# A shorter GpSimd chain, its powers queued on VectorE, the up projection's operands by halves, and the conditioning's rows written as rows

## The chip, the cores and the metric

One Trainium2 core runs the kernel. The metric is the device time in microseconds (us) of one execution. The engines named below are TensorE (PE in the profile), VectorE (DVE), ScalarE (ACT), GpSimd (POOL) and SyncE (SP), which issues most loads. Each engine runs its own instructions strictly in order; semaphores tie the engines together. ScalarE and GpSimd also issue DMAs (ACTq and POOLq in the profile), in the same order as their other instructions.

## The reference

One layer of a decoder trunk, on 1024 tokens of 1024 channels in float32. The conditioning vector c gives six rows of 1024 (shift, scale and gate, twice).

```python
ada = silu(c) @ w_ada + b_ada
sh1, sc1, g1, sh2, sc2, g2 = split(ada, 6)
h = modulate(x, sh1, sc1)
proj = h @ w_in
(xc, gc, gb, u_ssm, c_q, c_kv, k_r, g_conv, g_ssm, g_attn) = split(proj)
y_conv = (gb * causal_conv3(gc * xc)) @ w_up_conv
y_ssm  = glu(gelu(ssm(u_ssm))) @ w_up_ssm      # complex diagonal recurrence
y_attn = mla(c_q, c_kv, k_r, cos, sin) @ w_up_attn
y = (sigmoid(g_conv)*y_conv + sigmoid(g_ssm)*y_ssm + sigmoid(g_attn)*y_attn) @ w_o
x = layer_norm(a * x + g1 * y)
y = grouped_moe(modulate(x, sh2, sc2))
x = layer_norm(a * x + g2 * y)
```

The state-space branch has 32 groups of 64 complex states. Its step is lambda = exp(a*dt), a magnitude times (cos, sin) of an angle. The rotary tables cos and sin are of positions times inverse frequencies.

## The kernel before

A float32 product is made of three TensorE products of split operands (`mm3`, L137: low weights by high data, L140; high by low, L141; high by high, L142). `split_into` (L121) makes the high part by a cast on ScalarE (L125) and the low part by a subtraction on VectorE (L129). A projection tile of 128 channels by 1024 tokens is two halves of 512, each of 24 such matmuls.

The stages on TensorE follow each other in this order. The **front** (L480) normalises and modulates x and at once projects three of the four tiles of u, the state-space input; its order on VectorE, ScalarE and TensorE is written out by hand. `high(j)` (L570) makes the eight modulated slices on ScalarE, `low(j)` their low parts on VectorE. Behind it the **state-space stage** runs: u's tile 3 and five attention gates are projected (`proj_u`, `gates_att`), and between their matmuls stand the small ones of four quarters q of the state space (`s5_prep`, `s5_run`), of which each needs tables from GpSimd (X, T) and VectorE (G), a scan on VectorE and result rows Y that ScalarE takes from PSUM and SyncE writes to the array ys. Then `proj_qkv` (L876) projects the rotary key kr and the three tiles cq0 to cq2; its evacuation writes the buffers nt1, nt2 and nt3, and a table ctab is loaded from the array csd. Gates 5 to 7, moving sums and the paired projections follow (to about 585 us), then the **branches** (L1083: up projections of the convolution and the state space, with the rest of the conditioning's rows summed as they go by, `ada_rest`), attention, the merge, and the experts.

`s5_params` (L757) is GpSimd's long chain beside the front. It takes the exponentials of the step, one sine and cosine of 144 angles per partition (`sincos`: 16 of the state space and 128 of the rotary tables together), writes the rotary part to csd by four DMAs on ScalarE's queue (L789), makes lambda and the input factors, and squares the step's phase eight times (z8, L808 to L817). `s5_prep` makes a table T of 128 powers by seven doublings, six operations each, on GpSimd.

Outside the front and other stretches written by hand, a scheduler decides the order of each engine's instructions. The source order, the tile pools and `issue_after` (nothing of what follows is queued ahead of a given instruction) bound its choice. So the instruction order is shown below with the change.

## Time and profile before

| | us |
|---|---|
| median of 3 runs | 1539.91 (1537.67 to 1541.26) |
| profiled execution | 1540.56 |
| its span, first to last instruction | 1538.8 |
| TensorE busy | 1399.5 (91%) |
| VectorE busy | 914.3 (59%) |
| ScalarE busy | 483.4 (31%) |
| GpSimd busy | 373.6 (24%) |

TensorE is busy for nine tenths of the span, but its busy time is not the same as full speed: the mean clock granted to it is 0.960, and in single stretches it is 0.50. What other engines cost is therefore read from TensorE's waits and from the stretches behind them in which it runs at half clock.

### The profile page before, as it was taken

What the parts mean: (1) busy time and instruction counts of PE and PEld (TensorE: products, weight loads), DVE (VectorE), ACT (ScalarE), POOL (GpSimd) and SP (SyncE); (2) the same over time, 40 slices, a digit from 0 to 9 for tenths busy, and PEclk for the clock granted to TensorE, in tenths of its full rate; (3) what the DMA queues carried; (4) which work ended last, traced back from release to release, by engine and by line L of the source; (5) the groups of instructions that cost most, each with busy time, mean ns of one, the idle gap of its engine ahead of it and who ended that gap; (6) DMA issues with size and microseconds to landing.
All of it is one profiled execution on the core that took longest, in us unless ns stands there. A gap on an engine that the chain in (4) does not pass through costs nothing. (4 is left out here: it accounts for less than half of the span.)

```text
span 1538.8 us, 19602 instructions
## 1 busy us (share of the span) xinstructions
PE 1399.5 (91%) x6934; PEld 998.5 (65%) x6934; DVE 914.3 (59%) x1608; ACT 483.4 (31%) x869; POOL 373.6 (24%) x571
## 2 busy tenths in 40 slices
PE   4599797999999998999799997899988999999966
PEld 2477676888888886787587885688987333333322
DVE  7464687568765547557477887978886111122128
ACT  5232113522233334121367774333511111111103
POOL 7999930000000000004511143510032111111110
PEclk9899998999999998999899998999999999999988
DMA  9232222312133348869500005644635799778726
GB/s 371 104 117 85 77 56 42 122 64 83 55 109 110 110 151 329 249 203 215 84 1 15 15 22 188 206 172 172 250 139 200 276 340 347 289 264 308 239 104 259
DMA packets 78056, 251.61 MB, mean 164 GB/s; under 512 B 15946, under 2 KB 27266, under 8 KB 68739
## 3 DMA queue, kind: packets, MB, share of 16 engines
q1 hardware_dynamic: 54096, 203.61, 38.3%
q10 hardware_dynamic: 15506, 25.73, 4.8%
q0 software_dynamic: 8352, 20.98, 4.7%
q8 instruction: 56, 0.92, 0.2%
q14 instruction: 46, 0.37, 0.1%
HBM read 302.53 MB, written 50.38 MB: 229 GB/s over the span
## 5 line engine op out<-in xcount | busy, mean ns | idle before, releaser
L1143 POOL TENSOR_TENSOR mg<-mg,sg 128x512 f32<-128x512 f32 x16 | 22.5, 1418 | 491.1 <-DMA raw<-krd 474.6
L140 PE MATMUL ps_mm<-hh,wlo 128*128 128x512 f32 x304 | 123.0, 405 | 9.4 <-DVE nt L895 8.6
L1636 PE MATMUL ps_h<-wo,xt 128*64 128x512 f32 x480 | 130.9, 596 | 0.0
L142 PE MATMUL ps_mm<-hh,whi 128*128 128x512 f32 x304 | 123.3, 405 | 0.0
L141 PE MATMUL ps_mm<-hl,whi 128*128 128x512 f32 x304 | 122.5, 403 | 0.0
L1629 ACT COPY xt<-ps_tr 128x512 f32<-128x512 f32 x48 | 28.1, 585 | 244.8 <-PE ps_tr L1627 244.8
L1636 PE MATMUL ps_y<-wo,ht 128*64 128x512 f32 x288 | 87.6, 598 | 0.0
L1636 PE MATMUL ps_h<-ql,xt 128*64 128x512 f32 x192 | 87.0, 596 | 0.0
L125 ACT CAST whi<-raw 128x1024 fp32r<-128x1024 f32 (+1 forms) x45 | 46.8, 1040 | 126.6 <-PE ps_up L142 82.7
L129 DVE TENSOR_TENSOR wlo<-raw,whi 128x1024 fp32r<-128x1024 f32 x44 | 60.2, 1369 | 43.2 <-ACT whi L125 43.2
L1689 DVE TENSOR_TENSOR hd<-ps_h,hd 128x256 f32<-128x256 f32 x24 | 10.2, 424 | 126.9 <-ACT hd L1688 126.9
L140 PEld LDWEIGHTS ps_mm<-hh,wlo 128*128 128x128 f32 x304 | 58.8, 193 | 23.2 <-DVE nt L895 8.8
L1636 PEld LDWEIGHTS ps_h<-wo,xt 128*64 128x64 f32 x480 | 38.6, 137 | 49.6 <-issue 49.4
L142 PEld LDWEIGHTS ps_mm<-hh,whi 128*128 128x128 f32 x304 | 58.8, 193 | 14.6 <-issue 1.3
L141 PEld LDWEIGHTS ps_mm<-hl,whi 128*128 128x128 f32 x304 | 58.7, 193 | 13.3 <-issue 0.2
L1607 POOL DMA_INDIRECT xg<-h2d,idx x26 | 26.4, 1014 | 166.4 <-PE ps_tr L1627 137.4
L140 PE MATMUL ps_up<-ah,wlo 128*128 128x512 f32 x128 | 52.5, 418 | 10.1 <-ACT ah L125 7.5
L1664 DVE SCALAR_TENSOR_TENSOR y<-ps_y,roww,g 128x512 f32<-128x512 f32 x48 | 36.0, 751 | 38.8 <-PE ps_y L1636 38.8
L1249 DVE TENSOR_REDUCE sm<-ps_S 128x1 f32<-128x256 f32 (+3 forms) x64 | 49.2, 770 | 11.9 <-PE ps_S L1246 11.1
L129 DVE TENSOR_TENSOR pl<-ps_T,ph 128x512 fp32r<-128x512 f32 (+1 forms) x80 | 45.9, 580 | 14.5 <-ACT ph L125 13.2
L140 PE MATMUL ps_mm<-wo,ml 128*128 128x512 f32 x128 | 50.2, 400 | 3.1 <-DVE sg L1359 3.1
L141 PE MATMUL ps_up<-al,whi 128*128 128x512 f32 x128 | 52.0, 406 | 0.0
(676 smaller groups left out, 3878.8 us busy)
## 6 DMA issues: line engine op xcount, KB each, us to landing
wo<-exp SPq DMA_DIRECT2D x110, 1024.0 KB
qh<-exp SPq DMA_DIRECT2D x26, 1024.0 KB
ql<-exp SPq DMA_DIRECT2D x26, 1024.0 KB
raw<-w_in SPq DMA_DIRECT2D x43, 512.0 KB
adr<-w_ada SPq DMA_DIRECT2D x32, 512.0 KB
wada<-w_ada SPq DMA_DIRECT2D x16, 512.0 KB
fy<-yd SPq DMA_DIRECT2D x16, 512.0 KB
sga<-sg ACTq DMA_DIRECT2D x8, 512.0 KB
```

The lines of the kernel that those rows point to most:

```text
L125: nc.scalar.copy(out=hi, in_=src)
L129: e.tensor_tensor(out=lo, in0=src, in1=hi.bitcast(F32), op=ALU.subtract)
L140: mm(ps, wl, xh, start=first, stop=False)
L141: mm(ps, wh, xl, start=False, stop=False)
L142: mm(ps, wh, xh, start=False, stop=last)
L1143: nc.gpsimd.tensor_tensor(out=mg[m][:, sl], in0=mg[m][:, sl], in1=sg[:, sl], op=ALU.add)
L1249: v.tensor_reduce(out=sm[:], in_=x, axis=AX.XY if two else AX.X, op=ALU.max, negate=True)
L1607: self.nc.gpsimd.indirect_dma_start(out=self.xg[b % 2][:], out_offset=None, in_=self.h2d[:], in_offset=bass.IndirectOffsetOnAxis(ap=self.i ...
L1629: self.nc.scalar.copy(out=self.ex[b][:, n * 512:(n + 1) * 512], in_=ps[:])
L1636: self.nc.tensor.matmul(ps[z * 64:(z + 1) * 64, :], x[:, z * 64:(z + 1) * 64], w[z], start=first, stop=last, tile_position=(0, 64 * z))
L1664: nc.vector.scalar_tensor_tensor(out=y[:, sl], in0=ps[:], scalar=self.roww[:, b:b + 1], in1=self.g2[:, sl], op0=ALU.mult, op1=ALU.mult)
L1689: v.tensor_tensor(out=hd[:], in0=ps[:, 256:], in1=hd[:], op=ALU.mult)
```

## The change

It has six parts.

1. The 128 rotary angles leave the chain of `s5_params`: its sine and cosine have 16 columns. A new function `rotary`, called behind `s5_run(1)`, makes the tables on GpSimd in two buffers of u's ring (uq) and writes csd by four DMAs on GpSimd's own queue.
2. The powers z8 move from GpSimd to VectorE, behind the front's last `low`. Two small tables join them there: za (16 powers) and zb (8 powers), by four and three doublings.
3. T is one complex product of za and zb, six operations of 128x512, in place of seven doublings.
4. The evacuation of kr uses a ring of its own instead of nt1 and nt2, whose use stood behind ctab.
5. In the branches the first up weights are loaded and split ahead of the operands; the four operands are cast by halves, the very first half on VectorE; what follows is queued behind these casts until m is 1.
6. Each conditioning column [128, 8] is transposed on TensorE, copied by ScalarE to 8 rows of 128, and written as 8 rows of 512 bytes instead of 1024 single elements.

```diff
--- before
+++ after
                             prep.append(self.s5_prep(q + 2))
+                        if q == 1:
+                            self.rotary()
                     if self.stop == "s5":
...
             self.ada_col(col[:], self.aacc, 2 + c)
-            self.nc.scalar.dma_start(out=self.adad[c].rearrange("(j p) -> p j", p=128), in_=col[:])
+            ps, row = self.ps("mm"), P.tile([8, 128], F32, name="arow", tag="arow", bufs=2)
+            self.nc.tensor.transpose(ps[0:8, 0:128], col[:], self.ident[:])
+            self.nc.scalar.copy(out=row[:], in_=ps[0:8, 0:128])
+            self.nc.scalar.dma_start(out=self.adad[c].rearrange("(j p) -> j p", p=128), in_=row[:])
...
             for sl in (slice(0, 512), slice(512, S)) if j == 0 else (slice(0, S),):
-                v.tensor_tensor(out=self.hl[j][:, sl], in0=hts[j][:, sl], in1=self.hh[j][:, sl].bitcast(F32), op=ALU.subtract)
+                self.front_end = v.tensor_tensor(out=self.hl[j][:, sl], in0=hts[j][:, sl], in1=self.hh[j][:, sl].bitcast(F32),
+                                                 op=ALU.subtract).ins
...
         bb = self.bb
-        pos = P2.tile([128, 128], I32, name="pos")
-        nc.scalar.dma_start(out=pos[:], in_=bass.AP(a["positions"].tensor, 0, [[0, 16], [128, 8], [1, 128]]))
-        invf = t_("invf", 1)
-        nc.scalar.dma_start(out=invf[:], in_=a["inv_freq"])
         ar, ai, ldt = par[:, 0], par[:, 1], par[:, 2]
...
         self.exp_small(mag[:], t16[:], P2, [128, 16], v)
-        ang = t_("ang", 144)
-        v.tensor_tensor(out=ang[:, :16], in0=ai, in1=dt[:], op=ALU.mult)
-        v.tensor_copy(out=ang[:, 16:], in_=pos[:])
-        v.tensor_scalar(out=ang[:, 16:], in0=ang[:, 16:], scalar1=invf[:], scalar2=None, op0=ALU.mult)
-        sn, cs = t_("sn", 144), t_("cs144", 144)
-        self.sincos(sn[:], cs[:], ang[:], P2, [128, 144], v)
-        nsn = t_("nsn", 128)
-        v.tensor_scalar(out=nsn[:], in0=sn[:, 16:], scalar1=-1.0, scalar2=None, op0=ALU.mult)
-        csd = self.csd = self.dram.tile([2, 32, S], F32, name="csd")
-        for dst, src in ((csd[0, 0:16], cs[:, 16:]), (csd[0, 16:32], cs[:, 16:]), (csd[1, 0:16], nsn[:]),
-                         (csd[1, 16:32], sn[:, 16:])):
-            nc.scalar.dma_start(out=dst.rearrange("f (b t) -> (f b) t", b=8), in_=src)
+        ang = t_("ang", 16)
+        v.tensor_tensor(out=ang[:], in0=ai, in1=dt[:], op=ALU.mult)
+        sn, cs = t_("sn", 16), t_("cs16", 16)
+        self.sincos(sn[:], cs[:], ang[:], P2, [128, 16], v)
...
             v.tensor_tensor(out=self.m8[:], in0=self.m8[:], in1=self.m8[:], op=ALU.mult)
+        d = nc.vector
+        behind = ExitStack()
+        behind.enter_context(self.tc.issue_after(self.front_end))
         z = f("z8", 8, 2, 16)
-        v.tensor_copy(out=z[:, 0, 0], in_=cs[:, :16])
-        v.tensor_copy(out=z[:, 0, 1], in_=sn[:, :16])
+        d.tensor_copy(out=z[:, 0, 0], in_=cs[:, :16])
+        d.tensor_copy(out=z[:, 0, 1], in_=sn[:, :16])
+        self.za, self.zb = f("za", 2, 16, 16), f("zb", 2, 16, 8)
+        zt = t_("zt", 16, 8)
+        for x in (self.za, self.zb):
+            d.memset(x[:, 0, :, 0:1], 1.0)
+            d.memset(x[:, 1, :, 0:1], 0.0)
+        def double(x, n, i):
+            self.cmul(x[:, 0, :, n:2 * n], x[:, 1, :, n:2 * n], x[:, 0, :, 0:n], x[:, 1, :, 0:n],
+                      bc(z[:, i, 0], 2, n), bc(z[:, i, 1], 2, n), zt[:, :, :n], d)
         for i in range(9):
             src, dst = max(0, i - 3), max(0, i - 2)
             s0, s1, d0, d1 = z[:, src, 0], z[:, src, 1], z[:, dst, 0], z[:, dst, 1]
-            v.tensor_tensor(out=z[:, 7, 0], in0=s0, in1=s0, op=ALU.mult)
-            v.tensor_tensor(out=z[:, 7, 1], in0=s1, in1=s1, op=ALU.mult)
-            v.tensor_tensor(out=d1, in0=s0, in1=s1, op=ALU.mult)
-            v.tensor_scalar(out=d1, in0=d1, scalar1=2.0, scalar2=None, op0=ALU.mult)
-            v.tensor_tensor(out=d0, in0=z[:, 7, 0], in1=z[:, 7, 1], op=ALU.subtract)
+            d.tensor_tensor(out=z[:, 7, 0], in0=s0, in1=s0, op=ALU.mult)
+            d.tensor_tensor(out=z[:, 7, 1], in0=s1, in1=s1, op=ALU.mult)
+            d.tensor_tensor(out=d1, in0=s0, in1=s1, op=ALU.mult)
+            d.tensor_scalar(out=d1, in0=d1, scalar1=2.0, scalar2=None, op0=ALU.mult)
+            d.tensor_tensor(out=d0, in0=z[:, 7, 0], in1=z[:, 7, 1], op=ALU.subtract)
+        for n, i in ((1, 0), (2, 1), (4, 2), (8, 3)):
+            double(self.za, n, i)
+        for n, i in ((1, 4), (2, 5), (4, 6)):
+            double(self.zb, n, i)
         self.z8 = z
+        behind.close()
...
+    def rotary(self):
+        nc, a, v = self.nc, self.a, self.nc.gpsimd
+        us = [self.uqp.tile([128, 8, 128], F32, name="uq", tag="uq", bufs=2) for _ in range(2)]
+        room = [us[i // 8][:, i % 8] for i in range(16)]
+        names = {}
+        class P:
+            tile = staticmethod(lambda shape, dt, name, tag: names.setdefault(tag, room[len(names)]))
+        pos, ang, sn, cs = (P.tile(None, F32, n, n) for n in ("pos", "ang", "sn", "cs"))
+        pos = pos.bitcast(I32)
+        nc.scalar.dma_start(out=pos[:], in_=bass.AP(a["positions"].tensor, 0, [[0, 16], [128, 8], [1, 128]]))
+        invf = self.cst.tile([128, 1], F32, name="invf")
+        nc.scalar.dma_start(out=invf[:], in_=a["inv_freq"])
+        v.tensor_copy(out=ang[:], in_=pos[:])
+        v.tensor_scalar(out=ang[:], in0=ang[:], scalar1=invf[:], scalar2=None, op0=ALU.mult)
+        self.sincos(sn[:], cs[:], ang[:], P, [128, 128], v)
+        csd = self.csd = self.dram.tile([2, 32, S], F32, name="csd")
+        put = lambda dst, src: nc.gpsimd.dma_start(out=dst.rearrange("f (b t) -> (f b) t", b=8), in_=src)
+        put(csd[0, 0:16], cs[:])
+        put(csd[0, 16:32], cs[:])
+        put(csd[1, 16:32], sn[:])
+        v.tensor_scalar(out=ang[:], in0=sn[:], scalar1=-1.0, scalar2=None, op0=ALU.mult)
+        put(csd[1, 0:16], ang[:])
     def proj_u(self):
...
                                      stop=k == KT - 1 and i == 1)
-            t, k = half("nt1"), half("nt2")
+            x = self.ring("kr")
+            t, k = x[:, 0:512], x[:, 512:1024]
             nc.scalar.copy(out=t[0:64, :], in_=ps[64:128, :])
...
         T = f("T", 2, 4, 128, bufs=3)
-        tt = f("tt", 4, 64)
-        gp.memset(T[:, 0, :, 0:1], 1.0)
-        gp.memset(T[:, 1, :, 0:1], 0.0)
-        n, i = 1, 0
-        while n < 128:
-            self.cmul(T[:, 0, :, n:2 * n], T[:, 1, :, n:2 * n], T[:, 0, :, 0:n], T[:, 1, :, 0:n],
-                      bc(self.z8[:, i, 0, pr], 2, n), bc(self.z8[:, i, 1, pr], 2, n), tt[:, :, :n], gp)
-            n, i = 2 * n, i + 1
+        tb = lambda x: x.rearrange("p g (b a) -> p g b a", b=8)
+        za = lambda z: bc(self.za[:, z, pr], 2, 8)
+        zb = lambda z: bc(self.zb[:, z, pr], 3, 16)
+        self.cmul(tb(T[:, 0]), tb(T[:, 1]), zb(0), zb(1), za(0), za(1), tmp[:], gp)
...
-        if m % 2 == 0:
+        if m % 2 == 0 and self.upw is None:
             raw = self.load(src[m // 2].rearrange("p m k f -> p (m k f)"))
             self.upw = self.split(raw)
-        wh, wl = (w[:, (m % 2) * 512:(m % 2 + 1) * 512] for w in self.upw)
+        upw, self.upw = self.upw, None if m % 2 else self.upw
+        wh, wl = (w[:, (m % 2) * 512:(m % 2 + 1) * 512] for w in upw)
         for n in range(2):
...
         mg = [P.tile([128, S], F32, name=f"mg{m}") for m in range(KT)]
-        for t in range(4):
-            self.split_into(ah[t], al[t], self.load(self.cvd[t])[:])
+        self.upw = self.split(self.load(self.a["w_up_conv"][0].rearrange("p m k f -> p (m k f)")))
+        raws = [self.load(self.cvd[t]) for t in range(4)]
+        for n in range(2):
+            sl = slice(n * 512, (n + 1) * 512)
+            for t in range(4):
+                if n == t == 0:
+                    v.tensor_copy(out=ah[t][:, sl], in_=raws[t][:, sl])
+                else:
+                    hi = nc.scalar.copy(out=ah[t][:, sl], in_=raws[t][:, sl])
+                lo = v.tensor_tensor(out=al[t][:, sl], in0=raws[t][:, sl], in1=ah[t][:, sl].bitcast(F32), op=ALU.subtract)
+        behind = ExitStack()
+        for i in (hi, lo):
+            behind.enter_context(self.tc.issue_after(i.ins))
...
                 gelu(m // 2)
+            if m == 1:
+                behind.close()
         z = self.zp.tile([128, 4, S], F32, name="z")
```

(In the rows that follow, line numbers above the change's first hunk agree in both kernels, later ones are shifted: L577 and L583 are both `high`, L585 and L591 both `low`, L457 and L459 the same sigmoid, L1107 and L1155 the same gelu.)

**ScalarE at the end of the front.** Before, the four writes of csd stand between the sixth slice and the last two (hh_188 is slice 5's high part, hh_497 slice 6's); two of them are queued ahead of slice 6's `high`:

```order
L581 CAST hh_188<-ht 128x1024 [waits Activation_49]
L789 DMA csd<-sn 128x128 [waits DMAHW2_49,Pool_49]
L789 DMA csd<-nsn 128x128 [waits DMAHW3_49,Pool_49]
L577 ACTIVATE ht<-ps_x,col 128x512 [waits DVE_49,PE_49]
L577 ACTIVATE ht<-ps_x,col 128x512 [waits PE_49]
L789 DMA csd<-cs_662 128x128 [waits DMAHW4_49,Pool_49]
L789 DMA csd<-cs_662 128x128 [waits DMAHW5_49]
L581 CAST hh_497<-ht 128x1024 [waits PE_49]
L577 ACTIVATE ht<-ps_x,col 128x512 [waits DVE_49]
```

With the change the same place reads:

```order
L583 ACTIVATE ht<-ps_x,col 128x512 [waits DVE_49,PE_49]
L583 ACTIVATE ht<-ps_x,col 128x512 [waits PE_49]
L587 CAST hh_497<-ht 128x1024 [waits PE_49]
L583 ACTIVATE ht<-ps_x,col 128x512 [waits DVE_49]
L583 ACTIVATE ht<-ps_x,col 128x512 [waits PE_49]
L587 CAST hh_535<-ht 128x1024 [waits Activation_49]
L901 COPY uq<-ps_mm 128x8x64 [waits PE_49] x2
```

Slices 6 and 7 follow slice 5 directly, and no instruction there waits for GpSimd.

**VectorE behind the front.** hl_498 and hl_536 are the low parts of slices 6 and 7, wlo the low weights of u's tile 3, G a table of the state space. Before:

```order
L560 TENSOR_TENSOR col<-col,bias_180 128x2 [waits DVE_49]
L585 TENSOR_TENSOR hl_498<-ht,hh_497 128x1024 [waits PE_49,Activation_49]
L585 TENSOR_TENSOR hl_536<-ht,hh_535 128x1024 [waits PE_49,Activation_49]
L129 TENSOR_TENSOR wlo<-raw,whi 128x1024 [waits DMAHW2_49,PE_49,Activation_49]
L750 TENSOR_TENSOR G<-lam,cc 128x512 [waits DVE_49,Pool_49]
```

With the change, the rows from the last two low parts on:

```order
L591 TENSOR_TENSOR hl_498<-ht,hh_497 128x1024 [waits PE_49,Activation_49]
L591 TENSOR_TENSOR hl_536<-ht,hh_535 128x1024 [waits PE_49,Activation_49]
L805 COPY z_744<-cs_656 128x16 [waits Pool_49]
L806 COPY z_744<-sn 128x16
L811 MEMSET za 128x16
L812 MEMSET za 128x16
L811 MEMSET zb 128x16
L812 MEMSET zb 128x16
L820 TENSOR_TENSOR z_744<-z_744 128x16 [waits DVE_49]
```

and, 43 rows of the same kind further, the last ones ahead of tile 3's weights:

```order
L757 TENSOR_TENSOR za<-za,z_744 128x16x4
L824 TENSOR_TENSOR z_744<-z_744 128x16 [waits DVE_49]
L760 TENSOR_TENSOR za<-za,z_744 128x16x4
L823 TENSOR_SCALAR z_744<-z_744 128x16 [waits DVE_49]
L762 TENSOR_TENSOR za<-za,zt 128x16x2 [waits DVE_49]
L129 TENSOR_TENSOR wlo<-raw,whi 128x1024 [waits DMAHW1_49,PE_49,Activation_49]
```

The weights that TensorE needs for u's tile 3 now stand behind 55 small operations, of which the first waits for GpSimd's cosine.

**ScalarE where the branches begin.** sg is a gate's sigmoid, cv the gelu of a state-space row block, ah the high part of the convolution's operand. Before:

```order
L457 ACTIVATE sg<-sg 128x512 [waits DVE_49]
L1107 ACT_TABLE_LOAD [waits DMAHW3_49]
L1107 ACTIVATE cv<-raw 128x1024 [waits PE_49]
L1107 ACTIVATE cv<-raw 128x1024 [waits DMAHW6_49]
L459 DMA sgs<-sg 128x1024 [waits Activation_49]
L125 CAST ah<-raw 128x1024 x3
L125 CAST ah<-raw 128x1024 [waits DMAHW0_49]
```

With the change:

```order
L459 ACTIVATE sg<-sg 128x512 [waits DVE_49]
L461 DMA sgs<-sg 128x1024 [waits DMAHW6_49,Activation_49]
L1144 CAST ah<-raw 128x512 [waits PE_49]
L1144 CAST ah<-raw 128x512 [waits DMAHW4_49]
L1144 CAST ah<-raw 128x512 [waits DMAHW5_49]
L1144 CAST ah<-raw 128x512 x4
L1155 ACT_TABLE_LOAD
L1155 ACTIVATE cv<-raw 128x1024 [waits PE_49]
L1155 ACTIVATE cv<-raw 128x1024 [waits DMAHW2_49]
```

The seven half casts stand ahead of the activation table's load and the gelus.

## Rows read from the trace of the kernel before

**Rows 1.** Waits of TensorE, whole span: total, times, longest (us).

```profile
PE ps_x L568 <- ACT ht L577: 17.7, 2, 16.5
...
PE ps_mm L140 <- DVE nt L895: 8.6, 1, 8.6
...
PE ps_up L140 <- ACT ah L125: 7.5, 1, 7.5
PE ps_ss L972 <- POOL X L755: 6.1, 1, 6.1
PE ps_S L140 <- DVE qf L1214: 5.9, 1, 5.9
...
PE ps_up L140 <- DVE sg L1142: 2.6, 2, 2.0
```

**Rows 2.** Timeline of ScalarE, 72 to 80 us: start, duration, instruction, idle before.

```profile
74.42 0.78 ACT L577 ACTIVATE ht<-ps_x,col 128x512 f32<-128x512 f32 x1 [22.83 <-DMA csd<-sn]
```

**Rows 3.** Timeline of GpSimd, 38 to 75 us.

```profile
38.32 1.07 POOL L694 CAST ki<-k 128x16 int32<-128x16 f32 x1
...
58.67 0.22 POOL L691 TENSOR_TENSOR p<-p,r 128x16 f32<-128x16 f32 x1
...
74.24 0.49 POOL L746 TENSOR_TENSOR cs<-c,p 128x144 f32<-128x144 f32 x1
```

**Rows 4.** Timeline of TensorE at u tile 3's start, 88 to 91 us.

```profile
90.15 0.50 PE L140 MATMUL ps_mm<-hh,wlo 128*128 128x512 f32 x1 [0.79 <-DVE wlo L129]
```

**Rows 5.** Timeline of VectorE, 88 to 103 us.

```profile
88.42 1.67 DVE L129 TENSOR_TENSOR wlo<-raw,whi 128x1024 fp32r<-128x1024 f32 x1 [7.03 <-ACT whi L125]
90.02 0.70 DVE L750 TENSOR_TENSOR G<-lam,cc 128x512 f32<-128x512 f32 x1
...
100.68 2.19 DVE L755 TENSOR_TENSOR G<-G,xg 128x512 f32<-128x512 f32 x1
```

**Rows 6.** Groups of VectorE by shape, 0 to 60 us: busy us, mean ns, idle before.

```profile
L541 DVE TENSOR_TENSOR lnst<-lnst 128x2 f32<-128x2 f32 x2 | 0.3, 160 | 0.1
```

**Rows 7.** Timeline of VectorE in the state-space stage.

```profile
140.50 0.69 DVE L1025 TENSOR_TENSOR w<-ps_ss,T 128x512 f32<-128x512 f32 x1 [9.19 <-POOL T L752]
...
206.10 0.68 DVE L1025 TENSOR_TENSOR w<-ps_ss,T 128x512 f32<-128x512 f32 x1
...
230.27 0.69 DVE L755 TENSOR_TENSOR s<-s,xw 128x508 f32<-128x508 f32 x1
```

**Rows 8.** Timeline of TensorE in the state-space stage.

```profile
194.66 1.23 PE L1050 MATMUL ps_ss<-s,G 64*128 64x128 f32 x8
...
214.69 0.40 PE L140 MATMUL ps_mm<-hh,wlo 128*128 128x512 f32 x1
214.92 0.39 PE L141 MATMUL ps_mm<-hl,whi 128*128 128x512 f32 x1
...
243.97 0.80 PE L140 MATMUL ps_mm<-hh,wlo 128*128 128x512 f32 x1 [8.61 <-DVE nt L895]
```

**Rows 9.** Timeline of ScalarE where the branches begin.

```profile
588.07 3.79 ACT L1107 ACTIVATE cv<-raw 128x1024 f32<-128x1024 f32 x2
591.77 3.87 ACT L125 CAST ah<-raw 128x1024 fp32r<-128x1024 f32 x4
```

**Rows 10.** One stretch there: us, busy (x instructions) of PE, PEld, DVE, ACT, POOL; PEclk, DMA share, GB/s.

```profile
592.00:597.00 5.00, 4.14 (x9) 2.89 (x10) 5.00 (x5) 3.64 (x4) 0.00 (x0) 0.50 1.03 420
```

**Rows 11.** Two stretches behind the conditioning's writes, columns as above.

```profile
704.00:712.00 8.00, 8.00 (x37) 6.50 (x37) 7.96 (x8) 0.83 (x1) 5.60 (x6) 1.00 1.10 98
739.00:745.00 6.00, 5.44 (x24) 4.08 (x22) 1.21 (x2) 0.48 (x1) 1.98 (x3) 1.00 1.50 41
```

**Rows 12.** Timeline of ScalarE's DMA queue around the last of these writes.

```profile
738.99 0.37 ACTq L478 DMA_DIRECT2D adad<-acol  x1
...
744.57 1.10 ACTq L1176 DMA_DIRECT2D tab<-csd  x2
```

**Rows 13.** Timeline of VectorE at attention's start.

```profile
755.48 0.69 DVE L1214 TENSOR_TENSOR qf<-ps_S,tab 128x512 f32<-128x512 f32 x1 [5.89 <-DMA tab<-csd]
```

More of the change, by code (lines that the diff above doesn't have):

```diff
@@ L171, in build @@
             tc = self.tc
-            self.pst_ = None
+            self.pst_ = self.upw = None
             pool = lambda st, name, **kw: st.enter_context(tc.tile_pool(name=name, bufs=1, reuse_waits="tile", **kw))
```

## The prediction

> **What bounds the kernel now.** TensorE is busy for 1399.5 of 1538.8 us, so I read its waits first, then what the instruction behind each wait was itself waiting for, and last the stretches that follow, because TensorE often comes back from a wait at half clock. Six waits belong to places that the diff touches [rows 1]: 16.5 us in the front for `high`'s ht, 8.6 us for kr's nt, 7.5 us for the up projection's operand ah, 6.1 us for a table X of GpSimd, 5.9 us for a query qf, and 2.6 us for gates sg. The longest is not ScalarE's own work: its `high` started at 74.42 after 22.83 us of idleness that a DMA of csd ended, whose source is the sine [rows 2]. GpSimd's cosine came at 74.24 + 0.49 = 74.73 [rows 3]. So the front is bound by GpSimd's chain, through a queue and not through data.
>
> The wait for nt ends at 243.97 [rows 8], 13.0 us behind the last scan product of the fourth quarter (230.27 + 0.69 = 230.96, [rows 7]). The wait for ah ends behind two gelus of 3.79 us and the first of four casts of about 1 us [rows 9]. The one for qf ends with the table read from csd, issued at 744.57 and landed by 755.48 [rows 12, 13].
>
> **The change part by part: front.** No csd DMA stands ahead of slices 6 and 7 any more. TensorE's front ended 0.79 us before 90.15, at 89.4 [rows 4]; without the 16.5 us it ends at about 73. That gain doesn't pass on whole, for u's tile 3 needs its low weights, and these now stand on VectorE behind 55 small operations, the first of which needs GpSimd's cosine. When does that come? GpSimd's 128x16 operations take 0.22 us alone against 0.49 for 128x144, but 1.07 us beside VectorE's large ones [rows 3]. Some 31 wide operations lay in the uncontended part (about 57 to 74.7 us): 31 x 0.27 = 8.4 us less, 66.3. The two `low`s now fall into it (2 x 1.2 us in which GpSimd may be held up), so between 65 and 69; I take 67. The nearest rows to the 55 operations are VectorE's small ones of 160 ns with 0.05 us between them [rows 6]: 55 x 0.21 = 11.6 us, then the weights at 1.67 us [rows 5]. That gives 80.3. If GpSimd's own small operations were to alternate with them throughout, each would cost 0.21 + 0.22 and the start would be 67 + 23.7 + 1.7 = 92. I take 82, near the uncontended end, because a 16-column operation is short, and keep 79 to 92 for the range. Tile 3 then starts 8 us earlier than at 90.15.
>
> **State-space stage.** Here I count matmuls in the instruction order, from tile 3's first to the first quarters' last result: before, 275 wide ones and 147 others by the end of quarter 1's Y at 195.9 [rows 8]; now 332 and 179, because more of the filler is queued ahead. A wide one takes 0.23 us (214.92 - 214.69, [rows 8]): 0.2335 over longer stretches. Before: 195.9 - 90.15 = 105.7 us, less 64.2 for the wide ones and less the 6.1 us for X, leaves 35.4 us, 0.24 for each other one, small waits included. Now: 82 + 77.5 + 43 = 202.5. To this comes whatever TensorE waits for X. T's seven doublings (42 operations a quarter) become six operations of 128x512 at about 1.2 us, but some 80 rotary operations of 128x128 are queued between them, and VectorE no longer waits 9.19 us for the first T [rows 7]. GpSimd's load in this stage is therefore about the same, and I charge 3 us, with 0 and 10 as bounds: 205.5. Behind it the chain is serial as before: 2 us for the third quarter's state products, then VectorE's two quarters, which ran from 206.10 to 230.96 (24.9 us, [rows 7]), then 13.0 us until nt: 205.5 + 2 + 24.9 + 13.0 = 245.4. This wait stays in the program: with the change it is nt3 of cq2 that stands behind ctab on ScalarE. But kr's and cq1's matmuls are queued ahead of it, since kr no longer uses nt1 and nt2. That is 48 more wide matmuls than before, 11.2 us. The old kernel was at that point of its work at 243.97 + 11.2 = 255.2. **Gain of front and state space: about 10 us**; bounds 0 (tile 3 at 92) and 18 (tile 3 at 79, no X wait, and the chain covered so that only the 8.6 us remain).
>
> **csd and kr.** csd's four writes now wait on GpSimd's queue behind the rotary operations. ctab needs them. Its own wait for ys ended at about 242 before, and GpSimd's last work in this stage came earlier, so I charge nothing; if GpSimd ran late this cover would go, which is the slow rival below.
>
> **Branches.** The half casts move ahead of the table load and the gelus. The first half is on VectorE, free at once after the last gate; so the first up matmul waits about 1 us instead of 7.5. The stretch behind the wait ran at clock 0.50 for some 5 us [rows 10], a loss of about 2.4 us; a shorter pause should spare most of it. Against this, ScalarE's half casts (about 0.6 us by half of the row of rows 9) and the low parts pace the first sixteen products, and the gelus come later, but their results are wanted only behind the convolution's up projection. I take 8 us, with 4 and 10 as bounds.
>
> **Conditioning's rows.** Behind two of the four writes of single elements the DMA engines are full and move little: busy share 1.10 at 98 GB/s, then 1.50 at 41 GB/s [rows 11], against 420 GB/s in a full stretch [rows 10]. The last of them was issued at 738.99 on the same queue as the table, 5.6 us ahead of it [rows 12]; VectorE stood idle for 5.89 us until the table was there [rows 13], and TensorE with it. The gates' 2.6 us follow a like stretch, in which conditioning weights arrive late. With 8 rows of 512 bytes both causes go: 5.9 + 2.6 = 8.5 us, and about 1.5 for the half clock that follows such a pause. The four transposes have some 20 matmuls (5 us) between the column's sum and themselves, so TensorE does not wait for them; ScalarE waits for TensorE up to 5 us before its copy, and it has idle time there. I take 10 us, bounds 4 (the table still held by other loads) and 13.
>
> Sum: 10 + 8 + 10 = 28 us off the profiled 1540.6 gives 1512.6. The median lies 0.65 lower: **1512 us**. Work of attention and experts is untouched and moves ahead as a block.
>
> **A rule that speaks against it.** VectorE's subtraction of two tables of G took 0.70 us while GpSimd was on small work, and a like operation 2.19 us beside GpSimd's X [rows 5]. The Trainium skill (SBUF — State Buffer, section Who interferes with whom) says that a VectorE instruction with two SBUF inputs and a GpSimd instruction that reads SBUF lock each other out for a whole instruction, so that neither goes on beside the other. The trace agrees, with 2.19 against 0.70. By this rule the new squarings on VectorE alternate with lambda's operations on GpSimd, and tile 3 would start at 92 rather than 82: the first rival.
>
> **The rivals.** *The chain moves the stall instead of removing it* (0.22): tile 3 starts at 92 because the 55 operations run at 0.43 us each. Everything in the stage is 10 us later, gain 0 + 8 + 10 = 18: **1522**. For it speaks the 1.07 us of a 128x16 operation under load [rows 3]; against it that lambda has only some 30 operations. *More is gained* (0.15): upper bounds together, 18 + 10 + 13 = 41: **1499**. For it speaks that GpSimd had work without pause until the last T; against it that VectorE's 24.9 us chain remains. *Rotary holds up the tables* (0.08; slower): its 80 operations take 1.1 to 1.5 us each beside VectorE, as 128x16 ones did [rows 3], 40 to 80 us more on GpSimd, ahead of quarter 2's X. TensorE would wait at that X. To cancel the 28 us the wait must pass 28 + 3 = 31 us; at 40 us the time is **1550**. Against it: only VectorE operations with heavy traffic slowed GpSimd to that, and in this stage VectorE is busy for about half. *Half of the parts do nothing* (0.07): the branches wait for saturated loads and the table for other DMAs; only front and state space pay, 10 + 4 + 4: 1522 to **1535**.
>
> **How the numbers follow.** My forecast's own case (gain 22 to 33, 1507 to 1518) has 0.48. The range that leaves out no more than 2 in 10 goes from the fuller gain's middle, 1497, to **1532**. Faster by over 0.2% (3 us, about what a measurement of this kernel can tell) has 0.89, within 0.2% 0.04, slower 0.07.
>
> **What would show it.** Right: no wait over 2 us of `high` for a csd DMA; tile 3 starting near 82 behind VectorE's wlo; a remaining wait of 5 to 10 us near 245 in front of cq2's evacuation; a first up matmul within 2 us of the last paired one; no fall of GB/s behind the four writes, and qf not waiting for its table. Wrong: VectorE's small operations at over 0.35 us, TensorE waits of over 10 us for X, csd landing behind ys, or new waits of TensorE for a transposed column.

## The result, and the profile after

The changed kernel took 1518.45 us (median of 4 runs, 1515.91 to 1519.49), the kernel before 1540.59 beside it: ratio 0.9849, 95% interval 0.9825 to 0.9873. That is 22 us less; the prediction of 1512.0 us was 6.5 us too low and its range (1497 to 1532) holds the time. The profiled execution took 1517.72 us with a span of 1516.0; its mean clock is 0.963 against 0.960.

TensorE's waits after, whole span, columns as in [rows 1]:

```profile
PE ps_ss L1084 <- DVE s L759: 9.3, 3, 5.0
PE ps_ss L950 <- ACT nt L946: 8.1, 1, 8.1
...
PE ps_mm L140 <- DVE wlo L129: 6.7, 1, 6.7
...
PE ps_up L140 <- DVE mg L1165: 3.0, 1, 3.0
...
PE ps_v L140 <- DVE qf L1264: 2.1, 1, 2.1
...
PE ps_ss L1006 <- POOL X L762: 1.9, 2, 1.5
...
PE ps_S L140 <- DVE kl L129: 1.5, 1, 1.5
...
PE ps_v L140 <- DVE vv L129: 1.4, 1, 1.4
...
PE ps_up L140 <- DVE ah L1142: 1.2, 1, 1.2
...
PE ps_x L574 <- ACT ht L583: 0.8, 1, 0.8
```

The wait for ht (16.5 us) is 0.8, that for ah 1.2 instead of 7.5, those for qf and sg have shrunk. Against them stand waits that are new or longer: 6.7 us for tile 3's weights wlo (0.8 before), 9.3 for the scan's s (2.9 before) and 3.0 for the gated sum mg at the branches' start. The wait for nt is there as before, at 8.1. The front, by the timelines of GpSimd, VectorE and TensorE:

```profile
65.08 0.22 POOL L753 TENSOR_TENSOR cs<-c,p 128x16 f32<-128x16 f32 x1
65.34 0.18 DVE L805 COPY z<-cs 128x16 f32<-128x16 f32 x1 [2.35 <-POOL cs L753]
75.10 1.21 DVE L129 TENSOR_TENSOR wlo<-raw,whi 128x1024 fp32r<-128x1024 f32 x1
76.37 0.79 PE L140 MATMUL ps_mm<-hh,wlo 128*128 128x512 f32 x1 [6.66 <-DVE wlo L129]
```

The cosine is there 9.4 us earlier than in [rows 3], the 55 small operations fill 65.34 to 75.10 (0.18 us each on the mean, six of them 0.59 to 0.71), and tile 3 starts at 76.37 instead of 90.15: 13.8 us gained. Next, the state space, by the timelines of GpSimd, TensorE, VectorE and ScalarE:

```profile
97.79 0.69 POOL L716 TENSOR_TENSOR uq<-uq 128x128 f32<-128x128 f32 x1
...
131.22 1.28 POOL L762 TENSOR_TENSOR X<-X,xt 128x512 f32<-128x512 f32 x1
133.73 1.09 PE L1051 MATMUL ps_ss<-U,W 128*64 128x128 f32 x16
134.94 0.69 DVE L1059 TENSOR_TENSOR w<-ps_ss,T 128x512 f32<-128x512 f32 x1 [4.00 <-POOL uq L726]
...
158.06 0.80 PE L1084 MATMUL ps_ss<-s,G 64*128 64x128 f32 x4 [3.86 <-DVE s L759]
229.78 0.80 PE L1084 MATMUL ps_ss<-s,G 64*128 64x128 f32 x4 [4.99 <-DVE s L759]
230.39 0.69 DVE L762 TENSOR_TENSOR s<-s,xw 128x508 f32<-128x508 f32 x1
246.26 0.60 ACT L946 ACTIVATE nt<-ps_mm 128x512 f32<-128x512 f32 x1 [6.27 <-DMA ys<-Y]
246.91 1.87 PE L950 MATMUL ps_ss<-ones,nt 128*128 128x1 f32 x8 [8.07 <-ACT nt L946]
```

One of the rotary operations stands in the first row (uq is their buffer). VectorE's first w comes at 134.94, only 5.6 us earlier than in [rows 7]. The view names a rotary operation as its releaser, but w doesn't read uq: it reads the state product ps_ss, which ended at the same time (133.73 + 1.09), 2.3 us behind the end of X. The last s of the fourth quarter is there at 230.39 + 0.69 = 231.08, as late as in [rows 7] (230.96), and TensorE comes back from the wait for nt at 246.91. A table of stretches (us; busy of PE, PEld, DVE, ACT, POOL; PEclk, DMA share, GB/s) shows where it ran slower:

```profile
160.00:180.00 20.00, 20.00 (x114) 15.58 (x115) 12.25 (x12) 2.96 (x6) 16.63 (x16) 0.74 0.33 91
...
220.00:240.00 20.00, 13.30 (x88) 10.36 (x86) 13.97 (x25) 2.15 (x4) 0.11 (x1) 0.71 0.15 27
240.00:260.00 20.00, 13.09 (x62) 11.27 (x62) 10.62 (x17) 7.55 (x15) 0.00 (x0) 0.69 0.26 53
579.00:584.00 5.00, 4.57 (x16) 2.94 (x17) 4.35 (x8) 4.58 (x9) 0.00 (x0) 1.00 0.78 243
632.00:640.00 8.00, 8.00 (x36) 6.44 (x35) 5.46 (x5) 0.85 (x1) 0.00 (x0) 1.00 0.97 346
705.00:713.00 8.00, 8.00 (x36) 6.44 (x35) 6.84 (x7) 0.00 (x0) 5.08 (x4) 1.00 0.64 207
```

Behind each of the two waits for s (158.06 and 229.78) the granted clock falls to 0.74 and 0.71, means over 20 us in which the clock is partly full (2.4 GHz) and partly half (1.2 GHz). Where the branches begin it stays at 1.00 (0.50 in [rows 10]). The last two rows lie behind the first and the third of the conditioning rows' writes (issued at 630.02 and 696.56): the DMAs move 346 and 207 GB/s there at shares of 0.97 and 0.64, where [rows 11] has 98 GB/s at 1.10.

Last, the start of attention, by ScalarE's queue, VectorE and GpSimd:

```profile
725.62 0.27 ACTq L484 DMA_DIRECT2D adad<-arow  x1
726.27 1.10 ACTq L1226 DMA_DIRECT2D tab<-csd  x2
732.21 0.69 DVE L1264 TENSOR_TENSOR qf<-ps_S,tab 128x512 f32<-128x512 f32 x1 [0.82 <-POOL msk L1230]
735.46 2.35 POOL L129 TENSOR_TENSOR kl<-raw,kh 64x1024 fp32r<-64x1024 f32 x1
736.05 2.32 DVE L129 TENSOR_TENSOR ql<-qf,qh 128x512 fp32r<-128x512 f32 x1
739.77 0.69 DVE L129 TENSOR_TENSOR ql<-qf,qh 128x512 fp32r<-128x512 f32 x1
```

qf no longer waits for its table. But ql takes 2.32 us where it lies beside GpSimd's subtraction, and 0.69 us where it does not.

### The profile page after: what moved, and what is told of

The parts are those of the page before. It is cut to its first block, busy times and chain, and to the rows that moved or that the text cites. A ratio compares the mean times of both kernels' runs of the same rounds, so it can differ in the third digit from the quotient of the medians.

```text
span 1516.0 us, 19573 instructions
## 1 busy us (share of the span) xinstructions
PE 1400.5 (92%) x6938; PEld 998.9 (66%) x6938; DVE 936.2 (62%) x1706; ACT 484.7 (32%) x876; POOL 347.1 (23%) x426
## 5 line engine op out<-in xcount | busy, mean ns | idle before, releaser
L1193 POOL TENSOR_TENSOR mg<-mg,sg 128x512 f32<-128x512 f32 x16 | 23.4, 1472 | 474.8 <-DVE sg L1192 474.7
L141 PEld LDWEIGHTS ps_mm<-hl,whi 128*128 128x128 f32 x304 | 58.6, 193 | 13.8 <-issue 0.4
L1300 ACT ACTIVATE p<-ps_S,sm 128x256 f32<-128x256 f32 (+3 forms) x64 | 48.5, 758 | 10.8 <-DVE sm L1299 8.8
```

Of the source, the lines that this page charges most:

```text
L141: mm(ps, wh, xl, start=False, stop=False)
L1193: nc.gpsimd.tensor_tensor(out=mg[m][:, sl], in0=mg[m][:, sl], in1=sg[:, sl], op=ALU.add)
L1300: act.activation(out=y, in_=x, func=AF.Exp, bias=sm[:], accum_out=d)
```

## The experiments

Each kernel is given with its median in us, its ratio to the kernel before, measured on the same chip, and the 95% interval of the ratio. The kernel before has medians of 1534.9 to 1536.1 us beside the kernels of this section, but 1540.59 beside the changed kernel. A difference to the changed kernel therefore comes out some 5 to 7 us apart by the medians and by the ratios; where that matters both are given.

**What does each part give?** Three kernels: the kernel before with part 6 alone (the line that writes the column is replaced by the four of the change), with part 5 alone (the branches' hunks), and the changed kernel with parts 5 and 6 undone, which leaves parts 1 to 4.

```diff
--- before
+++ part 6 alone
-            self.nc.scalar.dma_start(out=self.adad[c].rearrange("(j p) -> p j", p=128), in_=col[:])
...
+            self.nc.scalar.copy(out=row[:], in_=ps[0:8, 0:128])
+            self.nc.scalar.dma_start(out=self.adad[c].rearrange("(j p) -> j p", p=128), in_=row[:])
```

> The kernel before with part 6 alone (the conditioning's columns transposed and written as rows of 512 bytes). Theory A, the forecast's term: both waits behind the writes (5.9 us for the table, 2.6 us for the gates) and the half clock behind them go, so 8 to 11 us are gained. Theory B: the writes' cost is real, but at the start of attention the next thing in line (VectorE's and GpSimd's low parts of the keys and queries) takes over most of the 5.9 us, as the changed kernel's trace suggests (TensorE idle 6.8 us there against 10.5 before); then 4 to 6 us are gained. Both: no fall of GB/s behind the writes, and qf's wait for its table gone.

> The kernel before with part 5 alone (up weights ahead, operands by halves, the rest queued behind). Theory A: 7.5 us of wait become about 1 and the half clock of the first 5 us goes, gain 8 us (7 to 10). Theory B: the gelus that now come later are missed further on (gate or state-space operands late, a wait of TensorE above 1 us between 600 and 700 us), and the gain is 5 us or less.

> The kernel before with parts 1 to 4 (front, powers, T, rotary, kr). Theory A: the stage gains what the changed kernel shows when the paired projections begin and end, 7 to 8 us, and the three pieces add up to the whole change's 22 us. Theory B: the pieces overlap, since the later stages of the changed kernel only move the same stall; then this one alone gives 12 us or more, or the three sum to more than 26 us.

Part 6 alone took 1533.37 us, 0.998 [0.9968, 0.9993]; part 5 alone 1526.61, 0.9939 [0.9922, 0.9956]; parts 1 to 4 together 1525.3, 0.9935 [0.9916, 0.9953]. By 1536 us these are 3, 9 and 10 us, together 22: the whole. The parts add up (Theory A of the last two), and only the conditioning's term is off (Theory B of the first, and less than its 4 to 6 us). Part 5 alone also shows Theory B's sign, a new wait of 1.9 us for mg at 605.32; its gain of 9 us is what is left with that wait. In the profile of parts 1 to 4, which still has the single-element writes, these are TensorE's waits at attention's start:

```profile
PE ps_S L140 <- DVE qf L1245: 4.7, 1, 4.7
PE ps_v L140 <- DVE vv L129: 1.4, 1, 1.4
...
PE ps_up L140 <- DVE sg L1173: 0.6, 1, 0.6
```

With the same old writes these waits are shorter here than in the kernel before (4.7 for qf against 5.9, 0.6 for sg against 2.6, [rows 1]); qf's is 5.3 with the ring alone and 4.5 with part 5 alone. With rows of 512 bytes qf no longer waits for its table, but in part 6 alone, as in the changed kernel, TensorE waits there 2.1 + 0.8 for qf and 1.5 for kl: the next in line took most of it. The half clock stayed too: from 740 to 760 and from 760 to 780 us the granted clock is 0.88 and 0.78 in the kernel before, 0.87 and 0.78 in part 6 alone.

**Which of parts 1 to 4 does it?** The ring for kr taken out of the changed kernel, and put alone into the kernel before:

```diff
--- after
+++ without kr's ring
-            x = self.ring("kr")
-            t, k = x[:, 0:512], x[:, 512:1024]
+            t, k = half("nt1"), half("nt2")
```

> The changed kernel with part 4 undone (kr's temporaries in nt1 and nt2 again). Theory A: the scheduler again has kr's evacuation behind the table's load, and with it cq1 behind the stall; TensorE loses the 48 matmuls of cover, so the kernel is slower than the changed one by 4 to 11 us. Theory B: the stall before the qkv evacuation is set by the scan's chain alone and shifts with it; kr's place makes no difference (within 2 us).

> The kernel before, with the ring for kr's evacuation alone. Theory A (the ring is a gain by itself: 48 matmuls, 11.2 us of work, move ahead of the place where TensorE waits 8.6 us for nt): that wait is under 2 us, and the time is 1526 to 1531 us, ratio 0.994 to 0.997. Theory B (the ring pays only where the front and the tables come earlier; here the matmuls that move ahead are taken from other waits of the stage): 1533 to 1538 us, ratio 0.998 to 1.001.

Without the ring the changed kernel took 1530.11, 0.996 [0.9943, 0.9976], 12 us more than with it by the medians and 17 by the ratios (Theory A, and more than its 4 to 11). The ring alone took 1522.7, 0.9916 [0.9894, 0.9938], which is 12 us from two lines, even beyond what Theory A allowed. TensorE's waits with the ring alone:

```profile
PE ps_x L568 <- ACT ht L577: 18.1, 1, 18.1
...
PE ps_ss L913 <- ACT nt L909: 1.7, 1, 1.7
```

and the timeline of TensorE in the changed kernel without it:

```profile
244.77 0.80 PE L140 MATMUL ps_mm<-hh,wlo 128*128 128x512 f32 x1 [8.79 <-DVE nt L932]
```

The ring takes the stall from 8.6 to 1.7 us although the front still waits its 18.1 us for ht. So parts 1 to 3, which take that wait away, gave nothing: with the ring 0.9935 against 0.9916 for the ring alone (the intervals overlap), and without it 0.996 against 0.9919 (0.9939 x 0.998, parts 5 and 6 alone), a loss of some 6 us by the ratios. The ten runs without the ring lie between 1523.8 and 1532.2, three of them below 1525, so the size of that loss is uncertain.

**Where did the front's 13.8 us go?** Three candidates: the wait for wlo, the csd tables' DMA in front of nt, and the rotary work on GpSimd's queue.

```diff
--- after
+++ tile 3's weights ahead of the powers
+                    self.w3_lo = nc.vector.tensor_tensor(out=self.w3[1][:], in0=raw[:], in1=self.w3[0][:].bitcast(F32), op=ALU.subtract).ins
+        behind.enter_context(self.tc.issue_after(self.w3_lo))
--- after
+++ ctab's load on GpSimd's queue
-        nc.scalar.dma_start(out=ctab[0:64, :], in_=self.csd[:].rearrange("z f t -> (z f) t"))
+        nc.gpsimd.dma_start(out=ctab[0:64, :], in_=self.csd[:].rearrange("z f t -> (z f) t"))
--- after
+++ rotary behind the third quarter's X
-                            self.rotary()
+                            with tc.issue_after(self.x2):
+                                self.rotary()
```

> The changed kernel with the weights of u's tile 3 loaded and split ahead of the small operations on VectorE, so that TensorE's 6.7 us wait for them goes. Theory A (work-bound up to quarter 1's result): the 5 to 6 us reach the end, gain 4 to 6 us over the changed kernel. Theory B (the powers' chain decides: T and with it the scan come later, by the 1.2 us that the subtraction takes): TensorE waits later for the first scan instead, and the gain is below 2 us.

> The changed kernel with ctab's load issued on GpSimd's queue instead of ScalarE's, so that the qkv evacuation on ScalarE no longer stands behind the wait for ys. Theory A: the 8.1 us wait of TensorE for nt is a queue effect like csd's in the front; it shrinks to about 2 us, and 5 to 8 us are gained with the half clock behind it. Theory B: nt itself lies in memory that the result rows Y hold until written, so the wait stays, within 1 us of the changed kernel.

> The changed kernel with the rotary tables queued behind the third quarter's X on GpSimd, out of the way of the first T and X. Theory A: the rotary operations between them delayed T and X, so w of the first quarter starts before 125 instead of 134.9, the waits for X (2.6 us) and for s (3.9 us at 158) go, and 4 to 8 us are gained. Theory B: the chain of the last two quarters sets the end whatever the first do, gain below 2 us; or csd comes so late (above 245 us) that ctab and the qkv evacuation wait for it, and it is slower.

Weights first took 1519.8, 0.99 [0.9879, 0.9921]: no gain, but 1 us more than the changed kernel by the medians and 8 by the ratios (Theory B). Tile 3 starts at 70.4, but TensorE waits 5.3 us for X, and T's first product on GpSimd, which came at 101.94 in the changed kernel, waits for zb:

```profile
110.28 1.09 POOL L760 TENSOR_TENSOR T<-zb,za 128x512 f32<-128x512 f32 x1 [2.58 <-DVE zb L762]
```

That is 8.3 us later, not the 1.2 us of a subtraction; the same edit is taken up again below, where the reason shows.

The table on the other queue took 1516.4, 0.9866 [0.9845, 0.9888], no measurable difference from the changed kernel. Theory A was right about the wait, for nt is early now and TensorE waits 1.7 us for it, but not about the gain: the next evacuation waits for the same write, and TensorE waits 3.6 us for cq. No data go from ys to cq, so the wait fits cq lying in memory that Y held, which is Theory B's reason:

```profile
247.16 0.58 ACT L947 COPY cq<-ps_mm 128x512 f32<-128x512 f32 x1 [4.92 <-DMA ys<-Y]
```

Rotary later took **1505.3 us** (1503.7 to 1506.03), 0.9796 [0.9779, 0.9812] (Theory A), clear of the changed kernel's interval and the fastest of all. The same places as in the profile after, by GpSimd's, TensorE's and VectorE's timelines:

```profile
117.87 1.26 POOL L763 TENSOR_TENSOR X<-X,xt 128x512 f32<-128x512 f32 x1
...
121.49 1.09 PE L1054 MATMUL ps_ss<-U,W 128*64 128x128 f32 x16
122.70 0.69 DVE L1062 TENSOR_TENSOR w<-ps_ss,T 128x512 f32<-128x512 f32 x1 [5.88 <-PE ps_ss L1054]
...
236.19 1.61 PE L951 MATMUL ps_ss<-ones,nt 128*128 128x1 f32 x8 [1.83 <-ACT nt L947]
```

X comes 13.4 us earlier, w 12.2, the last s of the fourth quarter is there at 219.70 instead of 231.08, and the wait for nt is 1.8 us at 236.19 instead of 8.1 at 246.91. The waits for X and s didn't go as Theory A had it: all those for s make 7.4 us against 10.7, those for X 1.4 against 2.6. The shorter wait for nt is the largest part of what TensorE got back. In the changed kernel 37 rotary operations, busy for 21.95 us, lie between 87 and 132.5 us on GpSimd (the table of that stretch for the buffer uq); here none lies ahead of that X.

**What does the late rotary leave to the others?** In this version the weights ahead once more, and kr's ring out:

> The version with the rotary tables behind the third quarter's X, and in it the weights of u's tile 3 split ahead of the powers on VectorE. Theory A (with the rotary work gone, GpSimd's tables come early enough that the 6.7 us that TensorE waits for these weights at the end of the front now pass on): 1499 to 1502 us, ratio about 0.976, the first state product 4 us or more earlier than its 141.8 us. Theory B (the powers come later by the weights' time, T and X with them, and TensorE waits for X what it no longer waits for the weights): 1504 to 1508 us, ratio about 0.980, and a wait for X of 4 us or more.

> The version with the rotary tables behind the third quarter's X, and in it kr's evacuation by nt1 and nt2 again, as before the change. Theory A (the four quarters end as TensorE's work ahead of them lets them, and the matmuls of kr and cq1 are the cover): the wait for nt is 7 us or more, and the time is 1512 to 1522 us, ratio 0.985 to 0.991. Theory B (with the tables early the last quarter is done before TensorE comes to that place, and the ring is not needed): 1504 to 1508 us, ratio about 0.980.

With the weights ahead the version took 1514.37, 0.9853 [0.983, 0.9875]: 9 us are lost, more than Theory B said, though TensorE's wait for wlo is gone. The timelines of VectorE and GpSimd say why:

```profile
74.85 1.21 DVE L761 TENSOR_TENSOR G<-lam,cc 128x512 f32<-128x512 f32 x1 [4.79 <-POOL lam L763]
...
79.71 1.07 DVE L825 TENSOR_TENSOR z<-z 128x16 f32<-128x16 f32 x1
...
106.22 1.10 POOL L761 TENSOR_TENSOR T<-zb,za 128x512 f32<-128x512 f32 x1 [15.37 <-DVE zb L763]
```

GpSimd's T waits 15.37 us for VectorE's powers (3.24 us in the version without this edit). VectorE itself was idle for 4.79 us until GpSimd's lam was there: with the weights ahead, the scheduler also put products of G, which need lam, ahead of the squarings. So the first squaring, at 65.60 in the changed kernel, comes at 79.71 here (and at 80.10 in the run with the weights first alone). Both runs show what a late chain of powers costs; what the weights ahead would give with the squarings in their old place is not shown. Without the ring the version took 1515.24, 0.9869 [0.9845, 0.9893] (Theory A): the ring is worth 10 to 11 us here too. Against 0.9919 for parts 5 and 6, parts 1 to 3 with the rotary late now give about 8 us by themselves.

**Where did the conditioning's 10 us go?** The split of kr's second copy moves off GpSimd at attention's start (in the version with the late rotary), and, in the changed kernel, each column is also written twice as single elements into a spare array:

```diff
--- rotary later
+++ kr's split on ScalarE and VectorE
-                                            hi_eng="pool", lo_eng="pool")}[x[0]](int(x[1]))
+                                            lo_eng="dve")}[x[0]](int(x[1]))
--- after
+++ eight writes of single elements added
+            for z in range(2):
+                self.nc.scalar.dma_start(out=self.sink[c, z].rearrange("(j p) -> p j", p=128), in_=col[:])
```

> The version with the rotary tables behind the third quarter's X, and in it the split of the second copy of kr at attention's start goes from GpSimd to ScalarE and VectorE. Theory A (what the conditioning's rows didn't give is lost there, since GpSimd's subtraction of 2.35 us stretches VectorE's ql to 2.3 us): TensorE's waits at attention's start for qf, kl and vv fall from 5.8 us to under 3, and the time is 1501 to 1503 us, ratio about 0.9775. Theory B (these waits are set by the order of the start and by ScalarE, and only change their names): they stay at 5 us or more, and the time is 1504 to 1507 us, ratio 0.979 to 0.981.

> The changed kernel, and behind each conditioning row two writes of the same column as single elements into an array that nobody reads: eight such writes, twice what the change removed. Theory A (the prediction's: such a write holds up the loads behind it and with them the gates, the table and the query, 10 us for four): about 20 us over the changed kernel, 1535 to 1540 us, ratio 0.997 to 1.0. Theory B (the loads are ahead of their use, and a write costs well under 1 us, as 2 to 3 us for four showed): 1518 to 1524 us, ratio 0.985 to 0.990.

With kr's split moved the version took 1505.76, 0.9797 [0.9775, 0.9819], no difference. VectorE's timeline:

```profile
723.71 1.21 DVE L129 TENSOR_TENSOR kl<-raw,kh 64x1024 fp32r<-64x1024 f32 x1
...
725.67 0.69 DVE L129 TENSOR_TENSOR ql<-qf,qh 128x512 fp32r<-128x512 f32 x1
```

ql is back at 0.69 us, but kr's own low part now stands ahead of it with 1.21; the waits for qf, kl and vv sum to 5.3 us against 5.8 (kl alone went from 1.5 to 2.6). Theory B holds.

With eight writes added the changed kernel took 1533.22, 0.9978 [0.9959, 0.9997], about 15 us more by the medians and 20 by the ratios (Theory A by its ratio). So a write of single elements does cost, and the prediction's mechanism is real. The loads behind it are late, as VectorE's timeline shows behind two writes issued at 627.48 (adr is a piece of the conditioning's weights):

```profile
641.73 1.28 DVE L271 SCALAR_TENSOR_TENSOR aacc<-adr,cond,aacc 128x1024 f32<-128x1024 f32 x1 [4.40 <-DMA adr<-w_ada]
```

VectorE's waits for such pieces sum to 23.4 us there and to 16.2 in the kernel before, and the changed kernel has none. TensorE's one wait for qf at attention's start is 5.4 us. A second way in which the added writes cost something is ScalarE's own queue: it is idle for 11.03 us until one of these writes has landed, and casts ah at 684.46 only (0.36 us of idleness at the same place in the changed kernel, at 668.22). The kernel before has no such wait, so the eight writes may cost more for that reason than the old four did. Each of the eight costs 1.9 to 2.5 us; each of the old four, by part 6 alone, 0.8.

## Why the prediction was right, and where it was off

**Front.** Right in its mechanism: no `high` waits for csd. cs came at 65.1 (67 taken, 65 to 69), the 55 operations took 9.8 us (11.6), tile 3 started at 76.4, earlier than the 79 of the range. Its rule against the change, that of the Trainium skill (SBUF — State Buffer, section Who interferes with whom), would have put tile 3 at 92; the operations of 16 columns don't show it on the whole, for six of the 55 took 0.59 to 0.71 us and the others 0.07 to 0.34. The larger ones do: 2.32 us for ql beside a GpSimd subtraction, 0.69 without. (The two rows of [rows 5] that the prediction calls subtractions are a product, L750, and a sum, L755.)

**State space.** -10 us was forecast and -10.0 measured for parts 1 to 4 (7 to 13 by the interval). Most steps stand: 2.6 us of waits for X (3 taken), the first quarters done at 201.7 (205.5), TensorE back at 246.9 (245.4). The chain behind it ran from 203.6 to 231.1, 27.5 us (24.9). Where the gain comes from stands in the sum, though not in the name "gain of front and state space": TensorE back at 245.4 is 1.4 us later than the 243.97 of the kernel before, and the 48 matmuls done by then make 11.2 - 1.4 = 9.8. So the whole term is the cover of part 4, the work that TensorE does while the chain that it will wait for goes on, and nothing of tile 3's earlier start is in it. The runs say the same: the ring alone gives 12 us, and the end of the four quarters (231 in both kernels) hadn't moved. The prediction didn't draw the conclusion that parts 1 to 3 buy nothing as they stand, and didn't ask why.

**The step that hid this** is "GpSimd's load in this stage is therefore about the same". The load was priced, though too high: the trace has 53 rotary operations and not some 80, and GpSimd's busy time over the whole execution fell from 373.6 to 347.1 us. Its place was not priced: 22 us of rotary work lay ahead of quarter 1's X, on which the state products and w depend. The rival "rotary holds up the tables" named the place, but looked for one long wait of TensorE at an X. Instead TensorE had projections queued ahead of that X and waited 0.46 us for it (at 132.56); it paid later, with waits for s of up to 5.0 us and for nt of 8.1, and with half clock behind them. Moving the rotary gave 8 us by the ratios and 13 by the medians.

**csd and kr.** "I charge nothing" for ctab's wait behind ys held: another queue for it changed nothing.

**Branches.** -8 us forecast, -9 measured; the first up matmul waits 1.2 us as said, and the clock stays at 1.00. The wait of 3.0 us for mg was not foreseen.

**Conditioning's rows.** This term was mis-sized: -10 us forecast, -3 measured (1.1 to 4.9 by the interval), with the median below the lower bound of 4. [Rows 11] already had the reason: behind the write, in 704 to 712 us, TensorE is busy for 8.00 of 8.00 us, so loads at 98 GB/s were still ahead of their use. The 5.9 us of qf were taken as a whole, though kl, vv and a second qf stood close behind, and the 1.5 us for the half clock didn't come, for the clock behind stayed as it was. That twice the writes cost 15 to 20 us fits loads whose lead covers one write and not two in a row, but it also fits ScalarE's wait of 11.03 us; the lead itself wasn't measured, and the two weren't told apart. A smaller part is that the waits of one trace were taken as the size, where other kernels with the old writes have 4.5 to 5.3 us for qf, as shown above. This term accounts for the 6.5 us between 1512 and 1518.

**Rivals.** "The chain moves the stall" (tile 3 at 92) didn't come; the stall did stay, for the reason above. "More is gained" needs the rotary later: that version is at 1505. The lower end of the range, 1497, is called the middle of that rival's gain, but the rival's own figure is 1499 and nothing gives 1497.

## What to carry to other kernels

Work that is moved off one critical chain must be placed in the queue where it lands: ask which instruction of that engine is wanted next, and queue it behind that. When TensorE stalls for a chain that cannot be shortened, matmuls freed to run ahead of the stall (here by two lines that give a buffer of its own) can be worth about what they take: here 11.2 us of matmuls gave 10 to 12 us by the medians, with three different chains. Price the removal of a wait down to the next wait in line, and read in the same row whether the bottleneck was busy behind the supposed cause.

## What was not expected of the hardware

The small writes and GpSimd's DMAs run on the same DMA engines at the same time. With the writes as rows the packets under 512 bytes between 725 and 740 us are 56, where the kernel before has 1103 between 738 and 756. The view of the DMA queues (queue: packets, MB, share of the engines' time), of the changed kernel and then of the kernel before:

```profile
DMA packets 321, 1.07 MB, mean 71 GB/s; under 512 B 56, under 2 KB 64, under 8 KB 320
...
q0 software_dynamic: 144, 0.52, 9.0%
```

```profile
DMA packets 1490, 1.61 MB, mean 89 GB/s; under 512 B 1103, under 2 KB 1103, under 8 KB 1488
q0 software_dynamic: 291, 1.06, 74.7%
q10 hardware_dynamic: 1197, 0.52, 17.0%
```

Most of the engines' time in that stretch of the kernel before goes to GpSimd's queue q0 (74.7%, 1.06 MB, the gated sums mgd), not to the small packets themselves (17.0%, with the table). The stretches are 18 and 15 us long, so by these rows q0 took about 12.7 us of all engines' time per MB in the kernel before and about 2.6 in the changed one. Why large packets take so long beside the small ones was not settled.

TensorE's clock can also be low in a stretch that is full: from 160 to 180 us it is busy for 20.00 of 20.00 us at a granted 0.74, behind one wait of 3.86 us, while the equally full stretch from 632 to 640 has 1.00. Read in stretches of 2 us, the granted clock is 0.50 from 158 to 170 us and 1.00 from 172 on.
